# Moving memory attention two blocks later and between the merge gates of a hybrid decoder layer

## The chip, the cores and the metric

The kernel runs on all 8 cores of one Trainium2 chip, which are two dies of four (cores 0 to 3 and 4 to 7). Every core has its own prompt sequence and its own 16 sample sequences; nothing passes between cores. The metric is device time in microseconds (us) of the slowest core. An execution is called slow when the cores of one die run at a lower clock than those of the other, or when it is over 1.5% above the fastest of the same kernel; only fast runs are compared here.

## The reference, cut to what matters

```python
h = rmsnorm(x)                                        # 17 tiles of 128 tokens a core, 1024 wide
u, v, p, q, gate_logits = split(h @ w_in)
a = gelu(u) * (tril(W_s) @ LN(gelu(v)) + b_s)         # within chunks of 128 tokens
b = pool_scale * (windowed_mean(p) - p) @ w_pool      # windows 2, 4, 8, 16
c = softmax(q @ K^T / 8) @ V                          # 4 heads, 256 memory tokens
#   prompt: K, V = rmsnorm(mem) @ w_kv;   sample (last tile): K, V from a cache in HBM
x = x + (sig(gA) * (a@Wa) + sig(gB) * (b@Wb) + sig(gC) * (c@Wc)) @ w_o
x = x + relu(rmsnorm(x) @ w_up)**2 @ w_down;  y = rmsnorm(x)
```

## The kernel before

One instruction stream per engine is written down in program order; a small scheduler puts in the semaphores. TensorE (PE), ScalarE (ACT), VectorE (DVE), GpSimd (POOL) and SyncE (SP) each run their own stream strictly in that order. The prompt goes through the first part in four blocks of four tiles. All matmuls share a ring of 8 PSUM banks, the buffers that PE writes its results to; a matmul group can start only when a bank of the ring has been read out. Helper names used below: `N(t)` normalises a tile on DVE, `T(t)` transposes it on PE and copies it into `hT`; `Q`, `P`, `V`, `U` are projections; `WIN` the pooling windows; `MIX` the spatial mixing; `S` the attention scores with their Exp, `AV` the weighted sum and the denominator; `SA1` to `SA3` the attention of the sample; `KV` makes keys and values from the memory tokens.

The start. `load_next(name, after=...)` asks on the POOL queue for the next 1 MB of weights, which are cast from fp32 to bf16 on the way; `after` names a load that must have landed first: `x_b[i]` is token tile i, `slot_b[i]` the i-th weight, `cst_b` a small table of constants.

```python
load_next("v", after=[x_b[0]])                # first weight: after token tile 0 has landed
for i in range(4):
    st_[i] = norm_a([i])                      # ACT: square and sum
    norm_b(*st_[i])                           # DVE and POOL: 1/sqrt
    if i == 2:
        load_next("pq", after=[x_b[2]])       # second weight: after token tile 2
    if i >= 1:
        N(i - 1)
        T(i - 1)
N(3)
load_next("u", after=[slot_b[0]])             # third weight: after the first has landed
gm, gm_b = mem_loads()                        # SP queue: memory tokens, 1.5 MB with their gain
load_x([4, 5, 6])
setup_loads()                                 # SP queue: rows for the fp32 setup matmuls
vmm(0); T(3); ...                             # V of block 0, then Q(0), P, WIN, U, setup_mm(), KV(), MIX, S, AV
```

A block of the first part and the merge loop after it:

```python
for j in range(1, 4):
    Q(j)
    vmm(i) ... vfin()                                  # V
    S(j, 0); S(j, 1)                                   # scores of this block
    if j >= 2: SA1(g0); SA1(g1)
    P(...), vout(...)
    if j >= 2: SA2(g0); SA2(g1)
    WIN(j)
    AV(j, 0); T(...); AV(j, 1); T(...)                 # with SA2b, SA3 between
    U(j, g) ..., MIX(j, g)
...
for m in range(8):                                     # merge: 128 output channels at a time
    for si, (c0, c1) in enumerate(SPLITS):             # 5 token ranges of 436 or 432
        # 3 gate matmul groups (24 matmuls) with a Sigmoid each, then
        # 8 matmuls of the branches, DVE multiplies, POOL adds
```

The softmax here doesn't subtract the row's maximum and nothing guards it: scores larger than these inputs give would overflow.

Of the kernel before, what the change touches and what calls it, by code (L numbers as in the profile page):

```python
# [186 lines left out]
def build_program():  # L187
# [30 lines left out]
    with st, nc.allow_non_contiguous_dma(reason="small strided rows"), \  # L218
# [14 lines left out]
        def Xt(t):  # L233
# [26 lines left out]
        kvs = [CRf[:, i * 4096:(i + 1) * 4096] for i in range(2)]  # L260
        kvs_b = [[s.buf("kvs%d_%d" % (i, a)) for a in range(2)] for i in range(2)]
        probs = CRf[:, 8192:12288].rearrange("p (a c) -> p a c", a=8)
        probs_b = [s.buf("probs%d" % i) for i in range(8)]
        hmT = CRf[:, 8192:10240].rearrange("p (k c) -> p k c", k=8)
        hmT_b = probs_b[0:4]
        qbd = CRf[:, 12288:13312].rearrange("p (f b c) -> p f b c", f=2, b=16)
        qbd_b = s.buf("qbd")
        prt = [CRf[:, 13312 + i * 512:13824 + i * 512] for i in range(5)]
        prt_b = [s.buf("prt%d" % i) for i in range(5)]
        bnds = CRf[:, 15872:17408]  # L270
        bnds_b = s.buf("bnds")
        cr_old = [(i * 4096 + a * 2048, i * 4096 + a * 2048 + 2048, kvs_b[i][a]) for i in range(2) for a in range(2)] + \
                 [(8192 + i * 512, 8704 + i * 512, probs_b[i]) for i in range(8)] + [(12288, 13312, qbd_b)] + \
                 [(13312 + i * 512, 13824 + i * 512, prt_b[i]) for i in range(5)] + [(15872, 17408, bnds_b)]
# [23 lines left out]
        wpo = [sb("wpo%d" % i, [128, 2, 128], BF16) for i in range(2)]  # L298
        wpo_b = [s.buf("wpo%d" % i) for i in range(2)]
# [108 lines left out]
        def norm_load(t, src):  # L408
            xt, xb = ring("xst", xst, xst_b)
            s.dma("sp", [(xt, src)], writes=[xb], owner=xb)  # L410
            norm_src[t] = (xt, xb)
# [7 lines left out]
        def norm_sq(nb, t):  # L419
            c, n, sb_, i = nb  # L420
            nb[3] += 1
            xt, xb = norm_src[t]
            xn, xnb = ring("xn", xnA, xnA_b)
            ACT(xn, xt, AF.Square, [xb], [xnb, sb_], accum_out=stats[:, c + i:c + i + 1])
            xn_of[t] = (xn, xnb, c + n + i, sb_)
# [36 lines left out]
        load_next("v", after=[x_b[0]])  # L462
# [35 lines left out]
        def tS(t):  # L498
            if t == 16:
                xn, xnb = ring("xn", xnA, xnA_b)  # L500
                return xn.bitcast(F32), xnb
            xt, xb = ring("xst", xst, xst_b)
            return xt[:, 0:512], xb
# [14 lines left out]
        pend = []  # L518

        def store(pairs, reads, owner):  # L520
            pend.append((pairs, reads, owner))

        def flush():
            for pairs, reads, owner in pend:
                s.dma("sp", pairs, reads=reads, owner=owner)
            pend.clear()
# [8 lines left out]
        def V(ts):  # L535
# [22 lines left out]
            def out(i):  # L558
# [8 lines left out]
                if t >= 15:  # L567
                    o = 0 if t == 15 else 1
                    (g0, g0_b), (g1, g1_b), (g2, g2_b) = [tS(t) for _ in range(3)]
                    s.dma("sp", [(g0[:], gbv[0:512].partition_broadcast(128))], writes=[g0_b], owner=g0_b)  # L570
                    s.dma("sp", [(g1[:], gbv[512:1024].partition_broadcast(128))], writes=[g1_b], owner=g1_b)
                    TS("dve", g2[:], gv[:], *sc, [gv_b, sb_], [g2_b])
                    TT("pool", g2[:], g2[:], g0[:], ALU.mult, [g2_b, g0_b], [g2_b])
                    TT("pool", g2[:], g2[:], g1[:], ALU.add, [g2_b, g1_b], [g2_b])
                    store([(cvo[o * 128:(o + 1) * 128, :], g2[:])], [g2_b], g2_b)
# [21 lines left out]
        def P(t):  # L597
# [8 lines left out]
            if t >= 15:  # L606
                po, po_b = tS(t)
# [81 lines left out]

        def S(j, hp):  # L690
            c0, c1 = hcols(j)
            for mc in range(2):
# [6 lines left out]
                for hh in range(2):  # L699
                    i = hp * 4 + hh * 2 + mc  # L700
                    ACT(probs[:, i, :], bks[hh][0][:, :], AF.Exp, [bks[hh][1]], [probs_b[i]], scale=0.125)

        def AV(j, hp):
# [3 lines left out]
            for mc in range(2):  # L707
                for hh in range(2):
                    h = 2 * hp + hh
                    i = hp * 4 + hh * 2 + mc  # L710
                    MM(bo[hh * 64:(hh + 1) * 64, :], v_p[:, mc, h * 64:(h + 1) * 64], probs[:, i, :], mc == 0, mc == 1, [vp_b, probs_b[i]], [bo_b])
            for mc in range(2):
                for hh in range(2):
                    i = hp * 4 + hh * 2 + mc
                    MM(bd[hh * 64:(hh + 1) * 64, :], ones, probs[:, i, :], mc == 0, mc == 1, [ones_b, probs_b[i]], [bd_b])
            rd, rd_b = tA()
# [11 lines left out]
        def SA1(g):  # L728
# [6 lines left out]
            pr, pr_b = tW()  # L735
# [40 lines left out]
        def mem_loads():  # L776
            gt, gt_b = ring("xst", xst, xst_b)
            s.dma("sp", [(gt, gvec[1].partition_broadcast(128))], writes=[gt_b], owner=gt_b)
# [4 lines left out]
            return gt, gt_b  # L783
# [20 lines left out]
        def WPO(m):  # L804
            wm, wb = slots[slot_of["mrg%d" % m]], slot_b[slot_of["mrg%d" % m]]
            wq, wq_b = wpo[m % 2], wpo_b[m % 2]
# [9 lines left out]
        def load_x(ts):  # L816
            for t in ts:
                norm_load(t, xrow(t))
# [5 lines left out]
        st_ = {}  # L824
        for i in range(4):
            st_[i] = norm_a([i])
            norm_b(*st_[i])
            if i == 2:
                load_next("pq", after=[x_b[2]])
# [4 lines left out]
        load_next("u", after=[slot_b[0]])  # L834
        s.dma("sp", [(bnd[:, B_CUR:B_SC], cb[:, B_CUR:B_SC])], writes=[bnd_b], owner=bnd_b)
        gm, gm_b = mem_loads()
        load_x([4, 5, 6])
        setup_loads()
        vmm(0)
# [4 lines left out]
        load_next("kv", after=[slot_b[1]])  # L844
        Q(0)
        for i in range(4):
            vout(i)
        mst = norm_a([100, 101])
        norm_b(*mst)
        for i in range(4):  # L850
            P(i)
        norm_c(100, gm, gm_b)
        norm_c(101, gm, gm_b)
        load_x([7])
        WIN(0)
        for t in range(2):
            trans(100 + t, hmT, hmT_b, t * 128, "dve")
        setup_ops()
        us = []
        na = norm_new(4)  # L860
        for g in range(4):
            us.append(U(0, g))
            norm_sq(na, 4 + g)
        norm_b(*na)
        setup_mm()
        KV()
        load_next("mrg0")
        N(4)
        N(5)
        for g in range(4):  # L870
            MIX(0, g, *us[g])
        S(0, 0)
        S(0, 1)
        T(4)
        N(6)
        T(5)
        N(7)
        load_x(BT[2])
        hst = hist_loads()
        AV(0, 0)  # L880
        T(6)
        AV(0, 1)
        T(7)
        hist_ops(*hst)

        for j in range(1, 4):
            nx = BT[j + 1] if j < 3 else []
            g0, g1 = 2 * (j - 2), 2 * (j - 2) + 1
            Q(j)
            vt = BT[j] + ([16] if j == 3 else [])  # L890
# [3 lines left out]
            for i in range(len(vt)):  # L894
# [3 lines left out]
                if j == 2 and i == 0:  # L898
                    norm_sq(na, 12)
                    norm_b(*na)  # L900
                if j == 2 and i > 0:
                    N(nx[i])
            if j == 2:
                N(nx[0])
# [3 lines left out]
            S(j, 0)  # L908
            S(j, 1)
            if j >= 2:  # L910
                SA1(g0)
                SA1(g1)
            for i in range(4):
                P(BT[j][i])
                vout(i)
            if j == 3:
                flush()
                P(16)
                vout(4)
            if j >= 2:  # L920
                SA2(g0)
                SA2(g1)
            if j == 3:
                load_next("mrg1")
                load_next("mrg2")
            WIN(j)
            if j == 1:
                N(nx[0])
                load_x([16])
                N(nx[1])  # L930
                load_x([13])
                kvs_load(0)
            if j >= 2:
                SA2b(g0)
            if j == 3:
                WIN(4)
            if j == 2:
                T(nx[0])
            AV(j, 0)
            if j == 1:  # L940
                N(nx[2])
                N(nx[3])
                load_x([14, 15])
            if nx:
                T(nx[0 if j == 1 else 1])
            if j >= 2:
                SA2b(g1)
            AV(j, 1)
            if nx:
                T(nx[1 if j == 1 else 2])  # L950
            if j >= 2:
                SA3(g0)
            if j == 2:
                kvs_load(2)
                kvs_load(3)
                T(nx[3])
            if j == 1:
                kvs_load(1)
                n16 = norm_new(1)
                na = norm_new(4)  # L960
            us = []
            if j == 3:
                u4 = U4()
            for g in range(4):
                us.append(U(j, g))
                if j == 1:
                    if g == 0:
                        norm_sq(n16, 16)
                        norm_b(*n16)
                        N(16)  # L970
                        load_x([12])
                    if g == 2:
                        norm_sq(na, 13)
                    if g in (1, 3):
                        T(nx[2 + g // 2])
            if j == 1:
                norm_sq(na, 14)
                norm_sq(na, 15)
                T(16)
                Q(4)  # L980
            if j >= 2:
                SA3(g1)
            if j == 3:
                WPO(0)
            if j == 3:
                load_next("mrg3")
            for g in range(4):
                MIX(j, g, *us[g])
# [272 lines left out]
```

## Time and profile before

| | before |
|---|---|
| time, median of 3 | 984.94 us (983.03 to 985.62) |
| profiled run, slowest core (1) | 994.5 us |
| profiled run, core 5 | 981.9 us |

From the page of the profiled execution (core 1): the busy row, the granted TensorE clock and the DMA share by slices (40 equal slices of the span, in tenths), and the chain of work that ended last.

```profile
PE 941.2 (95%) x5312; PEld 485.5 (49%) x5312; DVE 384.4 (39%) x644; ACT 291.1 (29%) x523; POOL 268.0 (27%) x274
...
PEclk9977778789999999999999999999999999999998
DMA  9954813078122221128023040400404022040034
...
PE 91%; DMA 4%; DVE 1%; SPq 1%; ACT 1%; issue 1%; POOL 0%; DVEq 0%; POOLq 0%; ACTq 0%
```

PE is the limit. The clock row shows something else: in slices 3 to 9, about 50 to 220 us, the core was granted 0.7 to 0.8 of the clock. In part that is peculiar to cores 0 and 1 of this execution: from about 55 to 217 us their clock records show 0.81 for most of the time, those of cores 2 to 7 never. The view of the cores:

```profile
core 1: 994.5 us, clock 0.957
...
core 5: 981.9 us, clock 0.984
```

Cores 2 to 7 took 972.7 to 982.4 us, which fits the timed 985, so core 5 stands for the kernel here. Its windows view splits the run at the first merge gate; columns are the stretch, its length, busy us and instructions of PE, weight load, DVE, ACT and POOL, granted clock, DMA share, GB/s.

```profile
0.00:200.50 200.50, 149.42 (x1242) 87.62 (x1243) 104.32 (x205) 85.79 (x157) 42.26 (x50) 0.93 0.56 125
200.50:981.90 781.40, 772.74 (x4074) 391.66 (x4070) 279.73 (x439) 204.61 (x366) 225.78 (x225) 1.00 0.25 59
```

After 200 us PE works without a gap, at full clock, until the tail. Before that it lacks 51 us of 200. The PE timeline of core 5 says where (start, length, engine, line, operation; in brackets the idle time before it and what ended it):

```profile
16.52 1.01 PE L344 MATMUL bank<-bnd,X 128*128 128x128 bf16 x8 [16.52 <-DVE X L359]
...
25.70 1.01 PE L344 MATMUL bank<-bnd,X 128*128 128x128 bf16 x8 [4.81 <-DVE X L359]
...
57.54 3.75 PE L341 MATMUL bank<-fW,CR 128*128 128x128 f32 x16 [4.01 <-DMA CR<-wpb]
...
81.37 3.61 PE L341 MATMUL bank<-hT,slot 128*128 128x512 bf16 x16 [2.49 <-DVE hT L365]
...
96.39 3.65 PE L341 MATMUL bank<-slot,hT 128*128 128x256 bf16 x32 [2.57 <-ACT CR L347]
...
120.57 0.61 PE L344 MATMUL bank<-bnd,X 128*128 128x128 bf16 x8 [2.22 <-ACT fA L347]
...
138.70 0.89 PE L341 MATMUL bank<-CR 128*32 128x256 bf16 x16 [1.54 <-ACT CR L347]
...
185.46 0.40 PE L341 MATMUL bank<-CR,fW 128*32 128x256 bf16 x8 [1.79 <-DVE fW L365]
```

The first two lines are the wait for tokens; the third is the wait for the setup rows; the fifth is P of block 1, which lacks PSUM banks because ACT still has to load a table and take eight Exp off the banks of the scores. Such gaps come to 34 us between the first matmul and the first gate. Two sums are used below: idle from the first matmul to the fp32 setup matmuls (the start; 12.2 us on the mean of cores 2 to 7), and from there to the first gate (the blocks; 19.9 us).

### The profile page before, as it was taken

The page shows a single profiled execution, that of the slowest core. Times are in us where ns is not written, and L with a number is a line of the kernel's source. Part 1 is how long each engine was busy: PE and PEld are TensorE (multiplying, and loading weights), DVE is VectorE, ACT ScalarE, POOL GpSimd, SP SyncE. Part 2 cuts the span into 40 slices and gives each one's busy share as a digit, 9 for nine tenths or more (in the row PEclk, how much of TensorE's full clock was granted, in tenths as well). Part 3 has the DMA queues.
Part 4 walks back from the last instruction along what each step waited for, and adds up shares of the span by engine and source line. Part 5 has one row for each costly group of instructions (what it writes and reads, how often), then busy time and mean ns, then how long its engine had stood idle before and what let it go on. Part 6 is the DMA issues. An engine that isn't in the chain of part 4 may idle for free.

```text
span 994.5 us, 15569 instructions; the slowest of 8 cores (972.7 to 994.5 us)
## 1 busy us (share of the span) xinstructions
PE 941.2 (95%) x5312; PEld 485.5 (49%) x5312; DVE 384.4 (39%) x644; ACT 291.1 (29%) x523; POOL 268.0 (27%) x274
## 2 busy tenths in 40 slices
PE   0878899899999999999999999999999999999996
PEld 0553555455555555554555544455445544455442
DVE  2644665432322233225541234322442224421476
ACT  2255542432222222223553300133002320033332
POOL 2130132143344334434333210133002220023243
PEclk9977778789999999999999999999999999999998
DMA  9954813078122221128023040400404022040034
GB/s 206 208 133 125 177 36 65 24 140 232 38 43 43 43 43 19 25 43 232 1 34 74 1 85 1 85 1 1 85 1 85 2 42 44 5 81 1 35 157 169
DMA packets 16969, 71.26 MB, mean 72 GB/s; under 512 B 2029, under 2 KB 3052, under 8 KB 13052
## 3 DMA queue, kind: packets, MB, share of 16 engines
q0 software_dynamic: 5472, 35.65, 21.1%
q1 hardware_dynamic: 11420, 34.61, 10.3%
q8 instruction: 44, 0.72, 0.3%
q14 instruction: 33, 0.27, 0.1%
HBM read 95.80 MB, written 10.22 MB: 107 GB/s over the span
## 4 chain that ended last, share of the span: by engine, by line
PE 91%; DMA 4%; DVE 1%; SPq 1%; ACT 1%; issue 1%; POOL 0%; DVEq 0%; POOLq 0%; ACTq 0%
PE bank L341 89%; DMA CR<-wpb 2%; DMA X<-x 2%; PE bank L344 2%; SPq L156 1%; DVE X L359 0%; ACT L347 0%; DVE hT L365 0%; ACT fA L347 0%; DVEq L128 0%; ACT CR L347 0%; ACT X L347 0%; DVE fA L359 0%; POOL stats L350 0%; POOL X L350 0%
## 5 line engine op out<-in xcount | busy, mean ns | idle before, releaser
L341 PE MATMUL bank<-hT,slot 128*128 128x436 bf16 (+3 forms) x2480 | 474.3, 352 | 3.4 <-DVE hT L365 3.4
L341 PEld LDWEIGHTS bank<-hT,slot 128*128 128x128 bf16 x2480 | 242.2, 99 | 221.8 <-issue 24.7
L341 PE MATMUL bank<-slot,CR 128*128 128x512 bf16 (+1 forms) x1376 | 298.9, 378 | 0.0
L347 ACT ACTIVATE fA<-bank 128x436 f32<-128x436 f32 (+2 forms) x219 | 119.0, 545 | 385.8 <-PE bank L341 372.1
L341 PEld LDWEIGHTS bank<-slot,CR 128*128 128x128 bf16 x1376 | 134.2, 98 | 157.2
L359 DVE SCALAR_TENSOR_TENSOR X<-bank,stats,X 128x512 f32<-128x512 f32 x136 | 102.1, 750 | 119.7 <-PE bank L341 119.7
L347 ACT ACTIVATE fW<-bank 128x436 f32<-128x436 f32 (+3 forms) x107 | 56.7, 532 | 175.5 <-PE bank L341 174.5
L350 POOL TENSOR_TENSOR CR<-fA 128x436 bf16<-128x436 f32 (+1 forms) x69 | 66.5, 964 | 108.6 <-ACT fA L347 104.6
L350 DVE TENSOR_TENSOR fA<-bank,fA 128x436 f32<-128x436 f32 (+1 forms) x77 | 43.0, 605 | 106.1 <-PE bank L341 102.7
L350 DVE TENSOR_TENSOR CR<-fA 128x436 bf16<-128x436 f32 (+1 forms) x51 | 31.2, 612 | 116.0 <-ACT fA L347 116.0
L350 POOL TENSOR_TENSOR stats<-stats,cstt 128x1 f32<-128x1 f32 (+3 forms) x30 | 35.7, 1189 | 130.4 <-DVE stats L356 99.8
L156 POOL DMA_DIRECT2D slot<-wpk x30 | 17.2, 573 | 182.8 <-PE bank L341 174.6
L341 PE MATMUL bank<-slot,hT 128*128 128x512 bf16 (+1 forms) x272 | 57.8, 384 | 2.6 <-ACT CR L347 2.5
L347 ACT ACTIVATE CC<-X 128x1024 bf16<-128x1024 f32 x34 | 35.9, 1057 | 76.1 <-DVE stats L356 36.8
L341 PE MATMUL bank<-X,slot 128*128 128x436 bf16 (+1 forms) x240 | 57.2, 347 | 0.0
L350 POOL TENSOR_TENSOR CR<-fW 128x436 bf16<-128x436 f32 (+1 forms) x37 | 35.1, 948 | 63.0 <-ACT fW L347 61.5
L350 DVE TENSOR_TENSOR fW<-bank,fW 128x436 f32<-128x436 f32 (+1 forms) x43 | 24.2, 605 | 58.8 <-PE bank L341 58.8
L341 PEld LDWEIGHTS bank<-slot,hT 128*128 128x128 bf16 x272 | 30.5, 113 | 28.3 <-issue 21.3
L350 POOL TENSOR_TENSOR fA<-fA 128x436 f32<-128x436 f32 (+1 forms) x22 | 24.3, 1104 | 71.8 <-DVE fA L350 71.8
L350 DVE TENSOR_TENSOR CR<-fW 128x436 bf16<-128x436 f32 (+1 forms) x29 | 17.8, 612 | 66.3 <-ACT fW L347 66.3
L344 PE MATMUL bank<-bnd,X 128*128 128x128 bf16 x152 | 15.1, 262 | 25.4 <-DVE X L359 23.2
L350 DVE TENSOR_TENSOR X<-bank,X 128x512 f32<-128x512 f32 (+1 forms) x35 | 23.9, 684 | 27.6 <-PE bank L344 14.5
(88 smaller groups left out, 495.6 us busy)
## 6 DMA issues: line engine op xcount, KB each, us to landing
slot<-wpk POOLq DMA_DIRECT2D x30, 1024.0 KB, 13.3
X<-x SPq DMA_DIRECT2D x34, 512.0 KB, 16.0
y<-hT SPq DMA_DIRECT2D x17, 512.0 KB, 2.6
CR<-ck POOLq DMA_DIRECT2D x4, 512.0 KB, 7.8
CR<-cv POOLq DMA_DIRECT2D x4, 512.0 KB, 9.7
gb<-gvec SPq DMA_DIRECT2D x3, 512.0 KB, 13.6
CR<-mem SPq DMA_DIRECT2D x2, 512.0 KB, 20.2
X<-gbv SPq DMA_DIRECT2D x4, 256.0 KB, 3.8
```

The lines of the kernel that those rows point to most:

```text
L156: eng.dma_start(out=o_ap, in_=i_ap).then_inc(owner.sem, 16)
L341: s.op("pe", lambda e: e.matmul(out, lhsT=lhsT, rhs=rhs, start=start, stop=stop), R_, W_)
L344: s.op("pe", lambda e: e.transpose(out=out, in_=in_, identity=identb), R_ + [ident_b], W_)
L347: s.op("act", lambda e: e.activation(out=out, in_=in_, func=func, **kw), R_, W_)
L350: s.op(eng, lambda e: e.tensor_tensor(out=out, in0=in0, in1=in1, op=op), R_, W_)
L359: s.op("dve", lambda e: e.scalar_tensor_tensor(out=out, in0=in0, scalar=scalar, in1=in1, op0=op0, op1=op1), R_, W_)
```

## The change

The intent is to take attention off the part of the program where PE waits for other engines, and to put it where it waits for none. Blocks 0 and 1 are attended in blocks 2 and 3, with projections around the scores; blocks 2 and 3 and the sample between the gates `G` and the branches `B` of the first merge steps. P goes before V, so that `WIN` finds its operands ready. `KV` goes to the end of block 1. Buffers are laid out anew in the shared region, so that the merge can write where attention is through. With this the start was rewritten too: other triggers for the weights (the first sooner, the second and third each after the one before), tiles 4 to 7 loaded and normalised earlier, the memory tokens loaded later.

```diff
-        load_next("v", after=[x_b[0]])
+        load_next("v", after=[cst_b])
 ...
         for i in range(4):
-            if i == 2:
-                load_next("pq", after=[x_b[2]])
             if i >= 1:
                 N(i - 1)
                 T(i - 1)
         N(3)
-        load_next("u", after=[slot_b[0]])
-        gm, gm_b = mem_loads()
-        load_x([4, 5, 6])
+        load_next("pq", after=[slot_b[0]])
+        load_x(BT[1])
         setup_loads()
+        mem_loads()
         ...
         vfin()
-        load_next("kv", after=[slot_b[1]])
+        load_next("u", after=[slot_b[1]])
+        na = norm_a(BT[1])
+        norm_b(*na)
         Q(0)
         for i in range(4):
+            P(i)
             vout(i)
 ...     (block loop: no S(j)/AV(j); instead, in block 2: S(0,*), AV(0,*), in block 3: S(1,*), AV(1,*))
-        for m in range(8):
-            for si, (c0, c1) in enumerate(SPLITS): ...
+        fill = {
+            (0, 0): lambda: S(2, 0),
+            (0, 1): lambda: S(2, 1),
+            (1, 0): lambda: AV(2, 0, tX),
+            (1, 1): lambda: (AV(2, 1, tX), S(3, 0)),
+            (2, 0): lambda: (S(3, 1), SA1(0), SA1(1)),
+            (2, 1): lambda: (AV(3, 0, tX), SA2(0), SA2(1)),
+            (0, 2): lambda: (AV(3, 1, tX), SA2b(0), SA2b(1), kvs_load(2), kvs_load(3)),
+            (1, 2): lambda: (SA3(0), SA3(1)),
+            (0, 3): lambda: (SA1(2), SA1(3)),  ...
+        }
+        for m, si in seq1b:          # three m at once while there is something to fill in
+            G(m, si)
+            if (m, si) in fill:
+                fill[m, si]()
+            B(m, si)
```

## The prediction

> **What bounds the kernel now.** TensorE. The profile's busy table has PE busy 941 of 994.5 us (95%); the chain of waits that ended last is 91% PE. That profile caught cores 0 and 1 at a lower clock (0.96 against 0.98; 990 and 994 us); the other six took 973 to 982 us, which fits the timed 985, so I read core 5 (981.9 us). From the first merge gate (200.5 us) to the last matmul (974 us) its PE timeline is solid at clock 1.00: 773 us that this change can hardly shorten. What is to be had lies before. PE starts at 16.5 us and then idles 34 us, in gaps that I add up from the timeline:
> - waiting for the first tokens: 7.2 us;
> - the setup loads before the fp32 setup matmuls: 4.0;
> - key/value preparation and block 0's scores: 2.8;
> - Q(1) behind the last token transpose of block 0: 2.5;
> - scores of block 1, holding PSUM banks through a table load (1.28) and eight Exp: 3.2;
> - pooling windows behind P's high/low split: 3.2;
> - transposes of blocks 2 and 3 behind normalisation: 5.2;
> - sample attention behind scores, and its evictions: 4.9;
> - the rest: 1.0.
>
> The windows table shows a granted clock of 0.74 to 1.0 between 40 and 200 us; busy time times (1 - clock) is about 11 us (7 to 14 on the undisturbed cores). The Trainium skill ("TensorE: Matmul & The Clock Gate", Part 1) says that idle windows of TensorE lower its clock; the trace agrees in that the clock dips only where the gaps are.
>
> **What the change does.** It removes almost no work; it moves. Attention of blocks 0 and 1 goes into blocks 2 and 3, with whole projections around the scores; attention of blocks 2 and 3 and of the sample goes between merge gates, where PE alone is the limit (ACT about 5.3, DVE about 6 of each 20 us). P goes before V, token transposes between U groups, memory loads and K/V off the start. It adds about 16 table loads in the merge: 16 x 1.28 = 21 us of ACT, in some 70 us of merge whose sigmoids take a quarter of ACT. "ScalarE: Activation LUTs" (What ACT_TABLE_LOAD costs) gives about 1283 ns; the trace has 1283. I expect ACT to absorb it; one step (AV plus scores) may lack a bank for under 1 us.
>
> **Sum (estimate from these durations).** Moved gaps: 2.8+2.5+3.2+3.2+5.2+4.9+4.0 = 25.8 us. New gaps: 3 us in blocks 2 and 3 (scores still wait for a table load before P gets banks), 2 for transposes, 1.5 in the merge: net 19. The clock loss falls from 11 to about 6: 5 more. The start stays load-bound (first 60 us: about 200 GB/s, DMA share near 0.9). Total 24 us: 985 - 24 = 961 us. Range 950 to 973. Faster by over 2% 0.64, within 2% 0.35, slower 0.01.
>
> **What would show it.** First merge gate at 165 to 172 us on an undisturbed core; PE idle between its first matmul and that gate near 14 us; clock there above 0.93; merge to end longer by the moved attention, 8 to 12 us, with no idle over 1.5 us; 20 or more table loads (10 before); no setup-load wait.
>
> **What would make it wrong.** Tokens 8 to 11 landing late, so ACT blocks in block 1; the earlier weight load delaying the first four token tiles; sample cache loads landing late in the merge; a denser first part meeting a lower granted clock, as cores 0 and 1 had (about 0.79).

## The result and the profile after

The changed kernel is correct and took 975.3 us (median of four runs, three fast: 973.25, 975.13, 975.47; one slow, 1124.52) against 985.28 before (there too one run of four is slow; the fast runs alone have medians of 975.13 and 984.94). The ratio is 0.9899, 95% interval 0.987 to 0.9928. Ratios here and below are the mean time of one kernel's fast runs over that of the other's of the same rounds, so they are not quite the ratio of the medians quoted. The gain is real, but 10 us instead of 24, and outside the range that was given.

The same rows of the page (core 7, the slowest):

```profile
PE 915.6 (94%) x5312; PEld 472.1 (48%) x5312; DVE 383.7 (39%) x644; ACT 306.2 (31%) x535; POOL 267.7 (27%) x274
...
PEclk9989999999999999999999999999999999999998
DMA  8891533804094122234050130402104040130134
...
PE 88%; DMA 5%; DVE 2%; ACT 1%; issue 1%; POOL 1%; DVEq 0%; SPq 0%; POOLq 0%; ACTq 0%
```

PE is busy for less time than before, in the same number of instructions, and its share of the chain went down. The clock row has one 8 in the first part instead of a row of 7s and 8s, which belonged to core 1 before. The windows view of core 7, cut at its first merge gate:

```profile
0.00:177.60 177.60, 131.87 (x1114) 77.25 (x1115) 96.86 (x175) 67.14 (x121) 37.48 (x45) 0.96 0.58 131
177.60:973.80 796.20, 783.78 (x4202) 394.83 (x4199) 286.83 (x470) 239.03 (x414) 230.20 (x230) 1.00 0.26 60
```

The first part is 23 us shorter than on core 5 before, the second 15 us longer. The PE timeline of core 7:

```profile
18.32 1.01 PE L347 MATMUL bank<-bnd,X 128*128 128x128 bf16 x8 [18.32 <-DVE X L362]
24.11 1.01 PE L347 MATMUL bank<-bnd,X 128*128 128x128 bf16 x8 [4.77 <-DVE X L362]
...
42.02 5.30 PE L344 MATMUL bank<-hT,slot 128*128 128x512 bf16 x16 [4.01 <-DMA slot<-wpk]
...
60.23 3.57 PE L344 MATMUL bank<-hT,slot 128*128 128x512 bf16 x8 [7.20 <-DMA slot<-wpk]
...
70.60 2.00 PE L344 MATMUL bank<-fW,CR 128*128 128x128 f32 x16
...
97.73 0.99 PE L347 MATMUL bank<-bnd,X 128*128 128x128 bf16 x8 [2.03 <-DVE X L362]
...
116.84 1.91 PE L344 MATMUL bank<-slot,hT 128*128 128x256 bf16 x16 [0.95 <-ACT CR L350]
...
207.71 0.53 PE L344 MATMUL bank<-X,slot 128*128 128x436 bf16 x2 [1.97 <-DVE X L353]
```

The third and fourth lines are new: Q(0) waited 4.0 us for the second weight, U(0) 7.2 us for the third. The fifth is the setup matmuls, no longer waiting for their rows but 13 us later than on core 5 before (8 on the means of the cores). The last is a merge step. The waits of PE, in total per releaser, on core 5 before,

```profile
PE bank L341 <- ACT CR L347: 6.3, 4, 2.6
PE bank L341 <- DMA CR<-wpb: 4.0, 1, 4.0
PE bank L341 <- DVE hT L365: 3.6, 2, 2.5
```

and on core 7 after:

```profile
PE bank L344 <- DMA slot<-wpk: 11.2, 2, 7.2
...
PE bank L344 <- ACT CR L350: 0.9, 1, 0.9
...
PE bank L344 <- DVE hT L368: 0.7, 1, 0.7
```

What was meant to go went (the Exp on the banks, 6.3 to 0.9; the token transposes, 3.6 to 0.7), and one new wait stands in its place. It is on all eight cores: 6.7 to 11.2 us, where before no core waited more than 2.5 us for weights. The table loads of ACT, before and then after, in count, busy us and mean ns:

```profile
L347 ACT ACT_TABLE_LOAD x10 | 12.8, 1283 | 29.7 <-PE bank L341 19.2 <-DMA X<-x 8.4 <-DVE X L365 2.0
L350 ACT ACT_TABLE_LOAD x22 | 28.2, 1283 | 19.1 <-PE bank L344 9.2 <-DMA X<-x 8.4 <-DVE fA L353 0.9
```

A balance of means over cores (before: cores 2 to 7, as 0 and 1 had the low clock; after: all eight). Idle times are added up from each core's PE timeline; for PE busy, cores with missing matmul records are left out.

| mean, us | before | after | difference | prediction |
|---|---|---|---|---|
| first matmul | 14.8 | 15.0 | +0.2 | 0 |
| PE idle in the start | 12.2 | 18.1 | +5.9 | -4.0 |
| PE idle in the blocks | 19.9 | 9.2 | -10.7 | -16.8 (from core 5's 21.7) |
| PE idle in the merge | 0.0 | 3.3 | +3.3 | +1.5 |
| PE busy (same instructions) | 921.7 | 914.9 | -6.8 | -5 |
| span of a core | 978.3 | 969.7 | -8.6 | -24 |

The idle time as a whole fell only from 32.1 to 30.6 us. Of the 15.4 us between the 24 that were forecast and the 8.6 that came, the start accounts for 9.9 and the blocks for 6.1. Most of what the profile shows as gained is that the same matmuls ran at a higher clock. The clock records bear this out: the busy time of PE, times what the clock lacked in it, adds up to a mean of 12.8 us before (cores 2 to 7) and 4.9 after. The Trainium skill ("TensorE: Matmul & The Clock Gate", Part 1) says that stretches without TensorE work lower its clock and sustained work restores it; the runs agree, in that core 5 before had six stretches at half the clock in its first part and core 7 after three (0.93 and 0.96 on the mean of that part), and that on core 7 it was 0.68 from 55 to 60 us, in which PE idled before U(0).

### The profile page after: what moved, and what is told of

It is laid out like the page before. It is cut to its first block, busy times and chain, and to the rows that moved or that the text cites. A ratio compares the mean times of both kernels' runs of the same rounds, so it can differ in the third digit from the quotient of the medians.

```text
span 973.8 us, 15566 instructions; the slowest of 8 cores (967.0 to 973.8 us)
## 1 busy us (share of the span) xinstructions
PE 915.6 (94%) x5312; PEld 472.1 (48%) x5312; DVE 383.7 (39%) x644; ACT 306.2 (31%) x535; POOL 267.7 (27%) x274
## 3 DMA queue, kind: packets, MB, share of 16 engines
q1 hardware_dynamic: 10988, 34.09, 10.7%
## 4 chain that ended last, share of the span: by engine, by line
PE 88%; DMA 5%; DVE 2%; ACT 1%; issue 1%; POOL 1%; DVEq 0%; SPq 0%; POOLq 0%; ACTq 0%
PE bank L344 87%; DMA slot<-wpk 3%; DMA X<-x 2%; PE bank L347 1%; ACT X L350 1%; DVE X L362 1%; POOL stats L353 1%; ACT L350 0%; DVE X L359 0%; DVE CR L362 0%; DVE X L368 0%; DVE stats L547 0%; SPq L156 0%; DVEq L128 0%; DVE X L353 0%
## 5 line engine op out<-in xcount | busy, mean ns | idle before, releaser
L344 PE MATMUL bank<-hT,slot 128*128 128x436 bf16 (+3 forms) x2480 | 471.1, 349 | 12.9 <-DMA slot<-wpk 11.2
L350 ACT ACTIVATE fA<-bank 128x436 f32<-128x436 f32 (+2 forms) x215 | 116.2, 544 | 361.6 <-PE bank L344 324.1
L350 ACT ACTIVATE fW<-bank 128x436 f32<-128x436 f32 (+2 forms) x103 | 54.7, 533 | 166.4 <-PE bank L344 164.7
L344 PE MATMUL bank<-slot,hT 128*128 128x512 bf16 (+1 forms) x272 | 48.4, 334 | 2.1 <-DVE fA L362 1.2
L353 DVE TENSOR_TENSOR X<-bank,X 128x512 f32<-128x512 f32 (+2 forms) x39 | 26.7, 685 | 49.9 <-PE bank L344 25.5
L344 PEld LDWEIGHTS bank<-slot,hT 128*128 128x128 bf16 x272 | 26.6, 100 | 21.6 <-issue 5.9
## 6 DMA issues: line engine op xcount, KB each, us to landing
slot<-wpk POOLq DMA_DIRECT2D x30, 1024.0 KB, 12.2
```

The costliest lines, as they stand in the source:

```text
L344: s.op("pe", lambda e: e.matmul(out, lhsT=lhsT, rhs=rhs, start=start, stop=stop), R_, W_)
L350: s.op("act", lambda e: e.activation(out=out, in_=in_, func=func, **kw), R_, W_)
L353: s.op(eng, lambda e: e.tensor_tensor(out=out, in0=in0, in1=in1, op=op), R_, W_)
```

## The experiments

Theory A: the loss is in the start, and comes of the chain of weight loads. Each is asked for only when the one before has landed. The POOL timeline shows the requests. Core 5 before:

```profile
8.21 0.74 POOL L156 DMA_DIRECT2D slot<-wpk  x1 [7.50 <-DMA X<-x]
...
20.10 0.57 POOL L156 DMA_DIRECT2D slot<-wpk  x1
...
25.94 0.57 POOL L156 DMA_DIRECT2D slot<-wpk  x1
```

Core 7 after:

```profile
5.51 0.73 POOL L156 DMA_DIRECT2D slot<-wpk  x1 [4.82 <-DMA cstt<-cst]
...
27.53 0.57 POOL L156 DMA_DIRECT2D slot<-wpk  x1
...
42.42 0.59 POOL L156 DMA_DIRECT2D slot<-wpk  x1 [1.10 <-DMA slot<-wpk]
```

The first weight is asked for 3 us sooner, but the second 7 us later and the third (u) 16 us later (on the means of the cores 2.8, 6.8 and 14.5). Part of the chain that ended last, core 7 after, in the critical view (start, length, what):

```profile
3.38 17.79 DMA X<-x
...
27.53 14.35 DMA slot<-wpk
...
42.42 17.68 DMA slot<-wpk
```

The chain begins with token tile 2 and not with a weight. The first weight had landed at 21.9 us, but the second was asked for at 27.5: its request stands on POOL behind the statistics of the token tiles, which came late. With the first weight asked for sooner, tile 2 landed at 18.5 us on the mean of the cores instead of 13.5 (in e4, where nothing else was changed up to then, at 19.4), and tile 3 at 21.2 instead of 18.2; the first weight itself landed at 20.4 instead of 22.6. Theory B: the bytes bind; whatever the order, the DMA engines are full (share 0.91 from 20 to 60 us on core 5 before). The windows view from 20 to 30 us speaks against it, core 5 before and core 7 after:

```profile
20.00:30.00 10.00, 5.19 (x29) 2.91 (x28) 4.01 (x5) 1.16 (x3) 2.77 (x4) 1.00 1.01 252
...
20.00:30.00 10.00, 3.70 (x21) 2.37 (x22) 5.08 (x8) 2.30 (x4) 3.55 (x3) 1.00 0.53 174
```

The DMA share (the last number but one) was 0.99 to 1.03 on the cores before and 0.53 to 0.87 after: in this stretch the engines ran short of requests. Theory C: the moved attention was worth less than reckoned, and the start is not the cause.

In the table, "setup at" is the start of the fp32 setup matmuls, as the mean over eight cores of the profiled run with its range, and "idle" the mean PE idle from the first matmul to there. Times are medians of fast runs.

| kernel | time, us | ratio to before | setup at, us | idle, us |
|---|---|---|---|---|
| kernel before (cores 2 to 7) | 984.9 | 1 | 57.0 (56.3 to 58.0) | 12.2 |
| changed kernel | 975.1 | 0.9899 | 65.3 (62.1 to 70.6) | 18.1 |
| e1_triggers | 973.1 | 0.9884 | 62.9 (60.5 to 65.6) | 14.4 |
| e2_mem_late | 970.2 | 0.9853 | 60.4 (58.0 to 62.4) | 13.5 |
| e3_both | 972.4 | 0.9875 | 62.2 (58.4 to 65.4) | 14.4 |
| e5_triggers_order | 970.1 | 0.9834 | 57.6 (54.2 to 59.8) | 11.5 |
| e6_order | 980.3 | 0.9946 | 67.4 (65.2 to 69.2) | 20.0 |
| e7_all | 970.7 | 0.9841 | 57.4 (54.4 to 58.9) | 11.5 |
| e9_norm_early | 967.9 | 0.9811 | 56.2 (54.7 to 58.9) | 12.8 |
| e10_norm_pq | 969.4 | 0.9835 | 56.3 (51.7 to 61.1) | 12.4 |
| e12_best | 965.7 | 0.977 | 54.9 (52.3 to 57.0) | 11.5 |

The ratios of e9, e10 and e12 are too low by 0.002 to 0.004, as some runs of the kernel before were disturbed on their chips; see e9 and e12. All changed versions, e4 too, keep the early request for the first weight; none puts that one trigger back, so what it costs by itself is not shown.

### e1_triggers: the old triggers for the second and third weight

```diff
             norm_b(*nb)
+            if i == 2:
+                load_next("pq", after=[x_b[2]])
 ...
         N(3)
-        load_next("pq", after=[slot_b[0]])
+        load_next("u", after=[slot_b[0]])
 ...
-        load_next("u", after=[slot_b[1]])
```

> The changed kernel with the old triggers for the second and third weight loads (p/q after the third token tile, u after the first weight has landed; first weight still early). Theory A (the changed kernel lost at the start because its weight loads run one after another: each is asked for only when the one before has landed): PE's waits for weight loads in the first 65 us fall from 7 to 11 us per core to at most 2, the first U matmul starts near 47 to 50 us (60.2 on the slowest core now), time 962 to 967 us against 975. Theory B (the same bytes have to come in before U(0) whatever the order, DMA share is near 1): the wait only moves to other loads (tokens 4 to 7, setup rows); time 971 to 976. Theory C (attention moves gave less than reckoned, the start is not the cause): 973 to 976 with the waits gone but new ones in blocks 1 to 3.

The weight waits went (at most 0.8 us on any core), as theory A said; the time fell by only 1.5 us (0.9884 against 0.9899), as theory B said. Three fast runs, 973.03 to 973.12; three more were slow. The wait had moved. ACT's timeline on core 4:

```profile
37.38 1.05 ACT L350 ACTIVATE X<-X 128x1024 bf16<-128x1024 f32 x1
...
41.84 1.06 ACT L350 ACTIVATE X<-X 128x1024 bf16<-128x1024 f32 x1 [2.08 <-DMA X<-x]
...
46.98 1.06 ACT L350 ACTIVATE X<-X 128x1024 bf16<-128x1024 f32 x1 [3.99 <-DMA X<-x]
...
48.03 1.19 ACT L350 ACTIVATE CR<-bank 128x256 bf16<-128x256 f32 x4
```

and PE's on the same core:

```profile
50.73 1.06 PE L344 MATMUL bank<-bnd,CR 128*64 128x16 bf16 x18 [6.53 <-DVE CR L353]
```

The first three lines are the squares of tiles 4, 6 and 7, which now land later because u is on the same engines. The fourth is ACT taking P of block 0 off its banks: it stands behind the squares in program order and waits for a tile that it does not need. So the windows waited 6.5 us. The Trainium skill ("TensorE: Matmul & The Clock Gate", the table of specifications at its head) says that ScalarE's and VectorE's queues are strictly first in, first out; this trace agrees, with 4.0 us spent on the last of these waits.

### e2_mem_late: the memory loads behind tiles 8 to 11

```diff
         setup_loads()
-        mem_loads()
 ...
         setup_mm()
         load_x(BT[2])
+        mem_loads()
```

> The changed kernel with the three memory loads (1.5 MB: gain and two memory tiles) issued behind tokens 8 to 11 instead of before them; weight triggers as in the change. Theory A: p/q's wait (about 4 us) stays, u lands only some 3 to 5 us sooner as it shares the engines with less: time 970 to 973. Theory B (bytes): 1.5 MB less at about 200 GB/s, 7 us sooner: time 966 to 969. In both the memory tiles must land before 88 us or block 1 stalls.

4.5 us gained (0.9853 against 0.9899); 970.2 us is at the edge of what theory A gave (970 to 973) and 1 us above what theory B gave. The wait for weights fell from a mean of 9.5 us to 3.4, and did so with the chain untouched: taking 1.5 MB out of the way made the chained loads faster. The Trainium skill ("DMA: Bandwidth & Descriptors", SWDGE vs HWDGE vs iDMA) says that requests from POOL and from SP go to different queues of the same DMA engines, which go round-robin between them; this run agrees as far as it can, since it moved only SP loads and sped up POOL's.

### e3_both: the two edits together

```diff
+    the diffs of e1 and e2
```

> Both edits. Theory A: as the triggers alone, within 3 us (959 to 966), since u then no longer waits. Theory B: as the late memory loads alone, 966 to 969.

972.4 us: no better than either (0.9875). This was expected by neither theory. The weight waits were gone (0.5 us on one core), the windows behind the squares again waited, for instance 6.5 us on core 1. With ACT's order as it was, asking for u early costs what it saves. Theory A alone falls here.

### e4_before_chain: the kernel before with the new triggers

```diff
-        load_next("v", after=[x_b[0]])
+        load_next("v", after=[cst_b])
-                load_next("pq", after=[x_b[2]])
-        load_next("u", after=[slot_b[0]])
+        load_next("pq", after=[slot_b[0]])
-        load_next("kv", after=[slot_b[1]])
+        load_next("u", after=[slot_b[1]])
 ...
+        load_next("kv", after=[slot_b[2]])
```

> The kernel before with nothing but the change's weight triggers (first weight after the constants, p/q after the first weight, u after p/q, k/v after u). Theory A: PE now waits for p/q and u here too, 5 to 11 us longer: 990 to 996 us. Theory B: same bytes, same time within 3 us (982 to 988).

991.4 us (four fast runs), ratio 1.0065 (1.0051 to 1.0079): 6.4 us slower, with 3.2 to 7.9 us of weight wait on every core (0 to 2.5 before). PE waits here for p/q and for k/v (on core 6, 3.6 and 4.1 us), for u at most 1.9 us, and in the start also longer for tokens: 8.0 us on the mean instead of 5.8. In this kernel the bytes are the same and the order of the requests alone costs; theory B in its plain form falls too. The edit moves all the triggers at once, the first with them, so it does not say which of them costs. Here ACT has P before the squares of tiles 4 to 7.

### e5_triggers_order: old triggers, and P before the squares on ACT

```diff
-        na = norm_a(BT[1])
-        norm_b(*na)
         Q(0)
         for i in range(4):
             P(i)
             vout(i)
-        N(4)
-        N(5)
+        na = norm_a(BT[1])
+        norm_b(*na)
         WIN(0)
+        N(4)
+        N(5)
 ...     (transposes of tiles 4 to 7 from behind U(0,0) to behind U(0,2); setup_ops after T(6); the k/v weights asked for before U)
```

> The run with the old triggers alone had no weight wait left (at most 0.8 us on any core) and still took 973: block 0's windows now waited 3.7 to 6.5 us, because ScalarE squares tokens 4 to 7 (now landing later) before it evicts P. This run adds to the old triggers: P evicted first, squares of tokens 4 to 7 after it, their transposes one U group later. Theory A2 (in-order ScalarE holds P behind late tokens): that wait falls below 1 us and the time to 966 to 969. Theory B (bytes bind, every wait moves on to the next consumer): waits move to the token transposes inside U(0) or to the setup rows, time 971 to 974.

970.1 us, ratio 0.9834: 6.4 us better than the changed kernel and about 5 better than e1. The windows' wait is down to 0.5 us, and the setup matmuls start 7.7 us sooner than in the changed kernel. What is left in front of them is 1.9 us for DVE to prepare their operand. The time came 1 us above the band that was written down, but the wait went where theory A2 said (in-order ScalarE holding P) and did not move on in full. With nothing outside the start changed against the changed kernel, the time is inside the range that was forecast for the change.

### e6_order: only the new order of block 0, above all on ACT

```diff
+    the lines shown for e5, on the changed kernel with its weight triggers
```

> The changed kernel with only that ScalarE order, weight chain kept. Theory A2: nothing, since u's landing still decides when U(0) starts: 973 to 976. If it gains over 3 us, the order and not the chain was the cause.

980.3 us: 4.6 us slower than the changed kernel. As expected there was no gain while U(0) still waited for u (6.2 us on core 5, and 3.7 for p/q). That it lost was not expected. The setup matmuls start 2.1 us later on the mean, but that need not come of the edit: e8, with the start of the changed kernel and on the same chip in the same rounds, started them at 67.4 us too. From gate to end it took 1.4 us longer than the changed kernel (e5 and e7, on this chip too, 2.0 and 1.5), and on cores 0 to 3 the clock records show short stretches at 0.81 there. Whether the edit by itself lost anything is not settled. What one chip and the same rounds do show is e6 against e5, which differ in the triggers alone: 980.3 and 970.1 us. With the order set, the old triggers are worth 10 us.

### e7_all: triggers, order and late memory loads

```diff
+    the diffs of e1, e2 and e5
```

> Old triggers, late memory loads and the ScalarE order together. Theory A2: 962 to 966, with PE idle between its first matmul and the setup matmuls near 10 us. Theory B: 968 to 971 as the late memory loads alone.

970.7 us, the same as e5 within the intervals (0.9841 and 0.9834). Idle in the start was 11.5 us, near the 10 expected, but not the time. Once u is asked for early and P is not held, the memory loads are not in the way.

### e8_premerge: all fills in one go before the first gate

```diff
+        for key in fill:
+            fill[key]()
+        fill.clear()
         for m, si in seq1b:
```

> The changed kernel with the whole attention of blocks 2 and 3 and of the sample run in one go before the first merge gate instead of between gates, same order. If placing it between gates is worth what the prediction said (scores and sums wait for a table load, eight Exp and evictions with nothing in between): 8 to 20 us slower, 983 to 995. Rival (the placement is worth little, block-level moves did the work): within 4 us of 975.

999.1 us, ratio 1.0131 (1.011 to 1.0152): by the ratios 23 us slower than with the fills between gates, and slower than the kernel before. This rules out that the placing is worth little, which is one part of theory C; that the moves were worth less than reckoned stays true of the blocks (10.7 us for 16.8, in the balance above). Idle in the blocks (which now hold the fills) was 24 to 30 us on the eight cores against 8 to 11. Waits of PE on core 1 from 170 to 240 us:

```profile
PE bank L347 <- ACT X L350: 8.2, 3, 5.7
PE bank L344 <- DMA CR<-ck: 6.5, 1, 6.5
```

The first is the transposes behind Exp, the second the sample's cache: the loads for its second half can only start when the first half is through, and between gates they are hidden. So part of the 23 us is that load and not the placing of the scores as such. Another part is the clock: PE was busy for 921.9 us with the same instructions, 7.0 more than in the changed kernel, at a clock of 0.91 to 0.93 in the first part instead of 0.95 to 0.97.

### e9_norm_early: normalise each of the first tiles at once

On top of e7. In the changed kernel DVE's stream has the statistics of tile i+1 before `N(i)`, so every tile waits for the next one's arrival.

```diff
             norm_b(*nb)
             if i == 2:
                 load_next("pq", after=[x_b[2]])
-            if i >= 1:
-                N(i - 1)
-                T(i - 1)
-        N(3)
+            N(i)
+            if i < 2:
+                T(i)
 ...
-        vmm(0); T(3); vmm(1); vmm(2); vmm(3)
+        vmm(0); T(2); vmm(1); T(3); vmm(2); vmm(3)
```

> The run with all three edits, and each of the first four tokens normalised as soon as its own square is there (in the change, VectorE waits for the next token's square first), with V's matmuls between the token transposes. If the start is held by that in-order wait: first V matmul near 21 to 23 us instead of 27, but then Q(0) waits for p/q (asked for at about 23 us): time 964 to 969. If the bytes alone decide when U(0) can start: no change from 970.7, within 2 us.

967.9 us, ratio 0.9811. V's first matmul starts at 19.2 us (core 1) to 22.3 us instead of some 27. On core 1 Q(0) then waits 3.0 us for p/q, as expected; on the seven others V itself waits 2.9 to 4.7 us for the first weight, which lands at 21.3 us on the mean. So weights hold PE for 5.5 us on the mean, and the setup matmuls start only 1.2 us sooner than in e7. The interval is wide (0.9742 to 0.988), because two of the seven runs of the kernel before on that chip took 994.5 and 997.65 us, the others 982.75 to 985.17; the four runs of e9 itself lie within 966.91 to 968.37. Against the five others (mean 984.0 us) the ratio is 0.9835, where e7 has 0.9841 on another chip: a gain over e7 is not shown by the times.

### e10_norm_pq: p/q one tile sooner

```diff
-            if i == 2:
-                load_next("pq", after=[x_b[2]])
+            if i == 1:
+                load_next("pq", after=[x_b[1]])
```

> As the run before, with p/q asked for after the second token instead of the third. If DMA idles at 20 to 30 us for want of requests (share 0.45 to 0.8 there now): p/q lands sooner, 960 to 966. If the engines are saturated: tokens 2 and 3 land later by as much, and the time is that of the run before, within 2 us, or worse.

969.4 us (three fast runs): no gain, rather 1.5 us worse. On the mean the setup matmuls start as in e9 (56.3 and 56.2 us), but over a wider range, 51.7 to 61.1 us, and the slowest core counts. The wait for p/q is gone on every core, but token tile 3 landed at 25.3 us on the mean instead of 22.3, and u, whose request stands behind that tile's statistics on POOL, was asked for at 27.4 us instead of 24.7. The wait for the first weight stayed (3.1 us on the mean, 3.3 in e9). In this part theory B holds: the DMA share from 20 to 30 us was 0.97 to 1.03, and what one load gained another lost.

### e11_fill_shift: the crowded merge step of the changed kernel split

In the changed kernel, merge step (1, 1) asks for 12 banks of the 8: 3 gates, 2 of AV, 4 of S, 3 branches. The timeline of core 2 there:

```profile
200.43 1.28 ACT L350 ACT_TABLE_LOAD   x1 [0.47 <-PE bank L344]
...
203.14 0.69 DVE L353 TENSOR_TENSOR X<-bank,X 128x512 bf16<-128x512 f32 x1 [4.74 <-ACT X L350]
...
203.98 0.53 PE L344 MATMUL bank<-X,slot 128*128 128x436 bf16 x2 [1.97 <-DVE X L353]
```

The last branch needs the bank of AV, which is free only after table load, Ln, Exp and the multiply on DVE.

```diff
-            (1, 1): lambda: (AV(2, 1, tX), S(3, 0)),
-            (2, 0): lambda: (S(3, 1), SA1(0), SA1(1)),
-            (2, 1): lambda: (AV(3, 0, tX), SA2(0), SA2(1)),
-            (0, 2): lambda: (AV(3, 1, tX), SA2b(0), SA2b(1), kvs_load(2), kvs_load(3)),
-            (1, 2): lambda: (SA3(0), SA3(1)),
+            (1, 1): lambda: AV(2, 1, tX),
+            (2, 0): lambda: (S(3, 0), SA1(0), SA1(1)),
+            (2, 1): lambda: (S(3, 1), SA2(0), SA2(1)),
+            (0, 2): lambda: (AV(3, 0, tX), SA2b(0), SA2b(1), kvs_load(2), kvs_load(3)),
+            (1, 2): lambda: (AV(3, 1, tX), SA3(0), SA3(1)),
```

> The changed kernel with one thing moved: the fill that put AV of block 2 and scores of block 3 into one gap (12 banks asked of 8, the 1.97 us wait on VectorE's output) is split over two gaps. Gate to end falls from 796 to 798 to about 793 to 794 and the time by 2 to 4 us, 971 to 973. If the wait only moves, within 1 us of 975.

From first gate to end it took 795.0 to 795.1 us on all cores instead of 796.1 to 798.0, with 2.1 us idle in the merge instead of 3.3. The time, 973.5 us, is 1.6 us below the changed kernel's, which was timed in other rounds, and the interval of the ratio (0.9811 to 0.9931) is too wide to call that a gain; against the five undisturbed runs of the kernel before there, the ratio is 0.9893. The gain is shown by the stretch in the profile alone.

### e12_best: e9 and e11 together

```diff
+    the diff of e9 (on top of e1, e2, e5) and that of e11
```

> The run with early normalisation (967.9) and the split fill together. The two lie in different parts of the program, so their gains should add: gate to end 795 instead of 797.8, time 964 to 967. If the merge gain is swallowed (another core or a clock dip takes over), 967 to 969.

965.7 us, the median of five fast runs (962.98 to 967.27; one slow), as expected. All eight cores of the profiled run took 956.8 to 961.3 us. The ratio is 0.977 (0.9703 to 0.9836), but it flatters: of the eleven runs of the kernel before on that chip, two had a whole slow die (1160 us) and five took 992 to 997 us. In these five, as in the two of e9's chip, one or two pairs of neighbouring cores had a clock of 0.957 to 0.963; in none of the 16 fast runs of changed kernels on these two chips (e9 to e12) did a pair fall so low. Why is not known. Against its four others (mean 984.4 us) the mean of 965.5 is a ratio of 0.981. This version is the fastest of all that ran, about 9 us faster than the changed kernel.

## Why the prediction was wrong

- **What bounds the kernel: right.** PE, with all that could be had in the first 200 us; from first gate to end before was 781.3 to 781.4 us on every undisturbed core.
- **The gaps of the blocks: right in kind, too large.** Reckoned was 21.7 to 4.9 us; measured was a mean of 19.9 to 9.2. The waits named are gone from the list, but transposes behind normalisation (2.0 us), the memory tokens' transposes and the first scores (about 1 us each) stayed. This shortfall of 6.1 us is read from the timelines; no run tests it.
- **The start: this step failed.** "The start stays load-bound (first 60 us: about 200 GB/s, DMA share near 0.9)", and in the sum the setup wait of 4.0 us as gained, with no term for what the new order of loads would cost. As averages the numbers held (share 0.87 to 0.95 in the first 60 us), but from 20 to 30 us the share fell to 0.53 to 0.87, and the loads that PE needs next came late. Idle in the start rose by 5.9 us instead of falling by 4.0: the setup wait went, but the third weight was asked for 14.5 us later on the mean, and PE waited 6.7 to 11.2 us for weights. e4 shows that the new triggers alone cost the old kernel 6.4 us. e1 and e5 show that undoing those of the second and third weight pays only together with the order on ACT: 1.5 us without it, 6.4 with it; e2 shows that the memory loads in between are part of it (4.5 us), and e3 and e7 that these gains do not add. The start was changed in several ways that depend on each other: the chain of weights, the memory loads, and the squares of tiles 4 to 7 before P. The risk list named "the earlier weight load delaying the first four token tiles", and this came true: tile 2 landed 5.0 us later on the mean and tile 3 3.0, with the request for the second weight behind them. The sum gave it no term.
- **The merge: mechanism right, size off.** Gate to end grew from 781.3 to a mean of 796.7 us: 3.3 idle instead of 1.5, and 12 of moved work (8 to 12 reckoned for both). Table loads rose from 10 to 22 and were absorbed. The step with AV and scores waited 1.97 us, not "under 1", as the bank comes free only behind DVE.
- **The clock: right, and somewhat larger.** PE busy fell by 6.8 us (5 reckoned), the loss in the clock records from 12.8 to 4.9 (11 to 6 reckoned), and the clock of the first part was 0.96 (core 7 after) against 0.93 (core 5 before).
- **The signs.** First gate at 169.1 to 177.6 us, not 165 to 172; PE idle between its first matmul and that gate 27.3 us on the mean, not near 14; no setup wait, as said.

What stays open: whether e6's edit by itself loses anything, what the early first weight alone costs, and how the last 11 us of idle in the start of e5 and e7 could go. Some 7.5 (e5) and 8.5 (e7) of them, on core 2, are still the wait for the first tokens, and 1.9 in each the operand of the setup matmuls; e9 takes most of the first away and gets waits for weights in its place.

## What to carry to other kernels

A high mean DMA share is no licence to ignore the order of loads: a load that is asked for only after another has landed can leave the engines short of requests, and a request also waits behind whatever stands before it in its engine's stream. So ask in the order of need, and check what an earlier request takes from the loads beside it: both early requests tried here, the first weight's and p/q's in e10, went with later token tiles. Every engine takes its stream in order, so one instruction that waits for a late load holds up those behind it that need nothing; when a load is moved, look at what stands behind its first reader. Work with long detours over other engines belongs where the limiting engine has plenty to do in between, and there the buffers that one step asks for at once should be counted against the ring.

## What the Trainium skill lacked or had wrong

- "TensorE: Matmul & The Clock Gate", Part 1, says to reckon with 13/16 of the clock for dense matmuls on all cores of a die. Here all eight cores ran matmuls nearly without a gap for 770 us, and in the profiled runs of the kernel before and the changed one the granted clock of that part was 1.00. A die at about that ratio for a whole run occurred only in some executions: in one slow run of e1 the cores of one die had clocks of 0.813 to 0.820 and took 1138 to 1147 us, those of the other die 0.99 and 963 to 970 us.
- "ScalarE: Activation LUTs", What ACT_TABLE_LOAD costs, gives about 2.66 us for a switch, with a drain. The load itself agrees (1283 ns); on core 5 before, the instruction ahead of a load ended at 94.34 us and the one behind it began at 95.65 us, 1.31 us in all.
- No page gives a figure for how much an early request on one queue delays loads under way on another: with p/q one tile sooner (e10), token tile 3 landed 3.0 us later, the mean start of the setup matmuls stayed where it was (56.3 us, 56.2 without) and its range over the cores went from 4.2 to 9.4 us. It would belong to "DMA: Bandwidth & Descriptors".
